# A hybrid decoder layer with one hand-placed SBUF map: no barriers, weights cast one stage ahead, the merge computed transposed

## The chip, the cores and the metric

The kernel runs on all eight cores of one Trainium2 chip, one batch element a core, no traffic between cores. The cores lie on two dies, 0 to 3 and 4 to 7. The time is the device time of the slowest core, in microseconds (us). Such a program has a second, slower state, in which the cores of a die get a lower TensorE clock.

## The reference, cut to what matters

One decoder layer over 4096 tokens of width 1024: gated linear attention (GLA, branch A) and dilated attention in three head groups (branch B) read one normalised input; a gated merge joins them; then cross-attention into 256 memory tokens, and a gated feed-forward with a short convolution. Cut marks are `...`:

```python
    xn = rms_norm(h, norm_mix)
    qa, ka, va, ra, za, qb, kb, vb = jnp.split(xn @ w_in, IN_OFFSETS, axis=-1)
    ...
    o_a = gla_chunked(heads(qa) * (GLA_DK ** -0.5), heads(ka), heads(va), heads(log_a))   # (B,H,S,dv)
    ...
    qd = rope_partial(rms_norm(dheads(qb), dil_q_norm), cos, sin)
    kd = rope_partial(rms_norm(dheads(kb), dil_k_norm), cos, sin)
    o_b = dilated_attention(qd, kd, vd).reshape(b, s, DIL_OUT).astype(dt)
    ...
    gates = jax.nn.sigmoid((xn @ w_merge_gate + b_merge_gate).astype(jnp.float32)).astype(dt)
    g_a, g_b = jnp.split(gates, 2, axis=-1)
    merged = g_a * (o_a @ w_br_gla) + g_b * (o_b @ w_br_dil)
    return h + merged @ w_mix_out
```

All weights arrive as f32; all matmuls are bf16. So each weight is converted once.

## The kernel before

Five stages, each with its own buffers, one behind the other. TensorE, VectorE (DVE), ScalarE (ACT), GpSimd (POOL) and the load queue (SP) each run their instructions in program order and wait on each other by semaphores; a helper records every operation, so the line numbers of the profile are the helper's, and tiles tell what is meant.

Weights are converted from memory to memory while GLA runs, one piece a chunk, each held by POOL until the chunk's output has been stored:

```python
        def emit_conv(after=None, n=1):
            ...
            if after is not None:
                fw.wait_for("pool", [after])
            fw.dma(d_, s_, q="pool", join=True)
        ...
        def R_t(c):                       # end of a GLA chunk
            ...
            fw.copy("act", oT[:, :, :], ptb.rearrange("p (c t) -> p c t", c=8))
            st_ins = fw.dma(oaT_d[c].rearrange("p (c t) -> p c t", c=8), oT[:, :, :], join=True)
            emit_conv(st_ins, 1)
```

Every stage ends in `fw.barrier()`: all engines wait for all engines and all transfers. The merge makes token rows, adds the gate bias as a matmul row, and transposes its result:

```python
        for kc in range(8):
            fw.mm(pg[:, :], xnv[:, kc, :], wmg[:, kc, gs_], start=(kc == 0), stop=False)
        fw.mm(pg[:, :], ones_row_b, bmg[0:1, gs_], start=False, stop=True)
        fw.act(ga[:, :], pg[:, :], AF.Sigmoid)
        ...
        for cc in range(8):
            fw.tr(ptb[:, cc * 128:(cc + 1) * 128], mr[:, cc * 128:(cc + 1) * 128], ident_b)
```

## Time and profile before

Median 3388.12 us of 3 runs (3384.28 to 3392.4). To keep books I cut the span of the profiled run at eight events, taken from their start times in the trace: the copies of a chunk's output (oT), of an attention tile's values (va), the last product of the merge (ma), the last query norm (qn) and the first copy of the feed-forward (abt).

| stretch | before, us |
|---|---|
| start to first GLA output copy | 100.9 |
| 24 GLA chunks | 458.1 |
| GLA chunk 24 to fourth attention tile | 175.8 |
| to last attention tile | 637.6 |
| to last merge product | 638.5 |
| to last query norm of cross-attention | 366.4 |
| to first feed-forward copy | 81.5 |
| to the end | 918.7 |
| span | 3377.5 |

A stretch is worth reading where TensorE is not full: rows one to three, and the places where one stage hands over to the next. The lines that carry this are in the prediction below.

### The profile page before, as it was taken

The numbers are of one execution on the slowest core, as the hardware profiler recorded it, in microseconds if no ns is written. First come the engines' busy times: TensorE is split into PE (matmuls) and PEld (weight loads), VectorE is DVE, ScalarE is ACT, GpSimd is POOL, SyncE is SP. The second block draws the span as 40 slices with busy tenths as digits, with TensorE's granted clock in tenths as the row PEclk, the third lists the DMA queues.
The fourth block names the chain that finished last, engine by engine and source line by source line (L and its number), as shares of the span: only waits on it lengthen the run. The fifth ranks groups of instructions, "written<-read, shape, count | busy, mean of one in ns | idle before, by whom it ended". The sixth has DMA issues, their size and how long they took to land.

```text
span 3377.5 us, 56089 instructions; the slowest of 8 cores (3357.1 to 3377.5 us)
## 1 busy us (share of the span) xinstructions
PE 3050.0 (90%) x18030; PEld 1535.8 (45%) x18030; DVE 1811.7 (54%) x3042; ACT 1386.0 (41%) x2679; POOL 868.2 (26%) x1284
## 2 busy tenths in 40 slices
PE   4887778699999999399999994999799999999998
PEld 2443344465555666244444442445344444444444
DVE  3665556467777767223333332576565566556554
ACT  2654445336666655234444442656321122112211
POOL 1332222236666666232222210000010011001100
PEclk8998889779999999699999997999899999999999
DMA  7678884021121111433333324134561101110110
GB/s 152 106 141 138 137 137 85 26 85 40 42 77 39 39 39 42 149 116 125 111 116 112 115 91 140 57 127 144 201 204 63 63 26 38 63 63 23 41 63 26
DMA packets 107503, 304.31 MB, mean 90 GB/s; under 512 B 12038, under 2 KB 24862, under 8 KB 104094
## 3 DMA queue, kind: packets, MB, share of 16 engines
q1 hardware_dynamic: 96702, 244.02, 21.3%
q0 software_dynamic: 8928, 50.93, 10.7%
q10 hardware_dynamic: 1584, 5.77, 0.5%
q8 instruction: 150, 2.46, 0.3%
q14 instruction: 139, 1.14, 0.1%
HBM read 258.92 MB, written 137.23 MB: 117 GB/s over the span
## 4 chain that ended last, share of the span: by engine, by line
PE 82%; DMA 7%; DVE 4%; issue 2%; ACT 2%; POOL 1%; SPq 1%; DVEq 0%; ACTq 0%; POOLq 0%
PE uP L170 27%; PE qP L170 16%; PE pj L170 15%; PE rP L170 9%; PE bP L170 6%; DMA oaT_d<-oT 4%; PE pS L170 2%; PE ptC L174 1%; PE ptC L170 1%; PE pO L170 1%; PE qP L174 1%; PE bP L174 1%; DVE on L229 1%; SPq L166 1%; PE rP L174 1%
## 5 line engine op out<-in xcount | busy, mean ns | idle before, releaser
L170 PE MATMUL uP<-x3T,wup 128*128 128x512 bf16 x2816 | 610.3, 380 | 0.0
L170 PE MATMUL pj<-wd,xnT 128*128 128x512 bf16 x2304 | 553.7, 384 | 2.1 <-DVE qg L203 2.1
L170 PEld LDWEIGHTS uP<-x3T,wup 128*128 128x128 bf16 x2816 | 275.9, 98 | 332.9 <-issue 1.7
L170 PEld LDWEIGHTS pj<-wd,xnT 128*128 128x128 bf16 x2304 | 253.0, 120 | 195.2 <-issue 8.1
L170 PE MATMUL uP<-wdn,yT 128*128 128x512 bf16 x1408 | 305.2, 379 | 0.0
L170 PE MATMUL qP<-wmg,xnT 128*128 128x512 bf16 x1024 | 241.9, 379 | 0.0
L239 POOL COPY hist<-abt 128x2 f32<-128x2 f32 x176 | 32.6, 185 | 808.2 <-ACT abt L238 808.2
L203 DVE TENSOR_TENSOR qg<-pj,gqk 128x512 f32<-128x512 f32 x192 | 132.8, 691 | 188.3 <-ACT sq L196 161.0
L170 PEld LDWEIGHTS uP<-wdn,yT 128*128 128x128 bf16 x1408 | 137.7, 98 | 166.2
L238 ACT COPY abt<-uP 128x512 f32<-128x512 f32 x176 | 100.2, 569 | 266.9 <-PE uP L170 266.9
L203 DVE TENSOR_TENSOR ma<-qP,ga 128x512 f32<-128x512 f32 x128 | 88.3, 690 | 203.0 <-ACT ga L196 200.8
L203 POOL TENSOR_TENSOR mr<-ma 128x1024 bf16<-128x1024 f32 x32 | 75.2, 2351 | 417.4 <-DVE ma L203 417.4
L196 ACT ACTIVATE pT<-pS 128x1024 bf16<-128x1024 f32 (+1 forms) x192 | 177.9, 927 | 4.5 <-PE pS L170 3.6
L196 ACT ACTIVATE sq<-pj 128x512 f32<-128x512 f32 x192 | 114.7, 599 | 151.0 <-PE pj L170 151.0
L196 ACT ACTIVATE ga<-qP 128x512 f32<-128x512 f32 x128 | 76.5, 598 | 228.1 <-PE qP L170 224.4
L203 DVE TENSOR_TENSOR h2f<-uP,h2f 128x512 f32<-128x512 f32 x64 | 44.3, 692 | 211.2 <-PE uP L170 210.4
L170 PEld LDWEIGHTS qP<-wmg,xnT 128*128 128x128 bf16 x1024 | 100.3, 98 | 120.9 <-issue 0.4
L196 ACT ACTIVATE gl<-cv_1 128x512 f32<-128x512 f32 x88 | 55.5, 631 | 222.6 <-DVE cv_1 L229 222.6
L196 ACT ACTIVATE gl<-cv_0 128x512 f32<-128x512 f32 x88 | 55.5, 631 | 219.3 <-DVE cv_0 L229 219.3
L229 DVE SCALAR_TENSOR_TENSOR cv_0<-abt,wcb,cv_0 128x512 f32<-128x512 f32 x176 | 132.2, 751 | 19.1 <-DVE cv_0 L229 0.5
L229 DVE SCALAR_TENSOR_TENSOR cv_1<-abt,wcb,cv_1 128x512 f32<-128x512 f32 x176 | 132.2, 751 | 18.3
L170 PE MATMUL bP<-wv,xnT 128*128 128x512 bf16 x512 | 132.6, 406 | 1.3 <-DVE ke_1 L203 1.3
(245 smaller groups left out, 5379.3 us busy)
## 6 DMA issues: line engine op xcount, KB each, us to landing
og_d<-og SPq DMA_DIRECT2D x96, 260.0 KB, 2.1
ogl<-og_d SPq DMA_DIRECT2D x96, 260.0 KB, 3.0
xt<-x SPq DMA_DIRECT2D x32, 512.0 KB, 7.9
xtT<-x SPq DMA_DIRECT2D x32, 512.0 KB, 4.8
h_d<-xtT SPq DMA_DIRECT2D x32, 512.0 KB, 2.9
h1x<-h_d SPq DMA_DIRECT2D x32, 512.0 KB, 5.5
h_d<-h1x SPq DMA_DIRECT2D x32, 512.0 KB, 3.6
h2f<-h_d SPq DMA_DIRECT2D x32, 512.0 KB, 6.1
```

Source lines behind the costliest of these rows:

```text
L166: return self._add(q, lambda e: e.dma_start(out=o, in_=i, **kw), [in_], [out], dma=True, join=join)
L170: return self._add("pe", lambda e: e.matmul(o, l, r, start=start, stop=stop), [lhsT, rhs], [out], xr=xr)
L174: return self._add("pe", lambda e: e.transpose(o, i, d), [in_, ident], [out])
L196: return self._add("act", lambda e: e.activation(o, i, func, **kw), reads, writes, xr=xr, xw=xw)
L203: return self._add(eng, lambda e: e.tensor_tensor(o, a, b, op), [in0, in1], [out], xr=xr)
L229: return self._add(eng, lambda e: e.scalar_tensor_tensor(o, a, scalar, b, op0, op1), reads, [out])
L238: return self._add("act", lambda e: e.copy(o, i), [in_], [out])
L239: return self._add(eng, lambda e: e.tensor_copy(o, i), [in_], [out])
```

## The change

Intent: one table of addresses in SBUF (the core's on-chip memory) for the whole kernel, in which each weight has a place that falls free one stage before it is needed. Then weights can be loaded with the conversion done on the way (called a cast from here on), a stage ahead; no barrier is needed, because each buffer inherits the waits of what lay there; and the tail of a stage can be interleaved with the head of the next. Besides, the merge makes its output already transposed (the bias is then one number per partition and rides in the activation), and the rotary tables are computed inside GLA. The host also lays weights and positions out in the order in which the loads take them, which the cuts below do not show.

The diff is long; its core, cuts marked:

```diff
+    def at(self, name, shape, dt, off):
+        assert off % 32 == 0
+        return self.register(Buf(self.handle(name, shape, dt, off), name), off, self.nbytes(shape, dt))
...
-            emit_conv(st_ins, 1)
...
-        emit_conv(None, 1000)
-        fw.barrier()
...
+        if c == NT - 1:                  # inside the last GLA chunk
+            c_alloc()                    # attention's buffers; load_wd(1), then gqk
+            for j in range(3):
+                proj(0, j)
+        R_on(c)
+        if c == NT - 1:
+            rope(0)
...
+        if c == 27:
+            c_early()                    # first attention weights wd0, tables
...
-                        fw.mm(pg[:, :], ones_row_b, bmg[0:1, gs_], start=False, stop=True)
-                        fw.act(ga[:, :], pg[:, :], AF.Sigmoid)
...
+        for kc in range(8):
+            fw.mm(pg[:, :], sl[:, gb + kc, :], xn[s_][:, kc, :], start=(kc == 0), stop=(kc == 7))
+        sg = T1["sg"].next()
+        fw.act(sg[:, :], pg[:, :], AF.Sigmoid, bias=bmg[:, br * 8 + m:br * 8 + m + 1])
...
+    kv_plan = {(4, 1): [lambda: kv_alloc(0), kv_alloc2, lambda: kv_norm(0)],
...
+        if 6 <= k < 19:
+            up_load(k - 6)
```

(`...` cuts; comments on the cut lines are mine.)

## The prediction

> **What bounds the kernel now.** I read the page first, to see which engine is full and where. Its slices, one digit for 84.4 us of the 3377.5 us span:
>
> ```profile
> PE   4887778699999999399999994999799999999998
> ...
> PEclk8998889779999999699999997999899999999999
> ```
>
> TensorE is full in the long stretches and holds a full clock there; it falls short in slices 1 to 8 and in dips at slices 9, 17, 25 and 29. The dips are the seams between stages, each behind a barrier. The view of busy time by stretch says whether another engine is near its limit (columns: stretch, length, then busy us of PE, weight loads, DVE, ACT, POOL, then granted clock, DMA share, GB/s):
>
> ```profile
> 320.00:392.00 72.00, 48.33 (x273) 25.16 (x272) 35.17 (x65) 25.51 (x58) 15.28 (x22) 0.83 0.86 136
> 559.00:615.00 56.00, 51.33 (x301) 26.63 (x302) 35.61 (x72) 28.19 (x66) 16.53 (x16) 1.00 0.10 30
> 900.00:1000.00 100.00, 100.00 (x905) 56.43 (x904) 72.13 (x130) 65.27 (x102) 67.22 (x85) 1.00 0.23 73
> 1600.00:1700.00 100.00, 100.00 (x523) 44.61 (x523) 35.82 (x53) 42.61 (x64) 24.58 (x16) 1.00 0.37 119
> ```
>
> These are the linear attention (GLA) with weight conversion running, the same four chunks' work without it, the dilated attention, and the merge. Attention and merge are TensorE at 100%. In GLA nothing is full while conversion runs, and TensorE takes 51 of 56 us when it has stopped. Who waits there is in the view of waits for 110 to 645 us:
>
> ```profile
> DVE on L229 <- POOL hs L203: 67.0, 20, 9.3
> POOL nss L221 <- ACT junkA L196: 83.9, 19, 7.6
> POOL w_ffn_up_bf L166 <- DMA oaT_d<-oT: 38.1, 3, 15.8
> ```
>
> POOL stands before a conversion's issue until the store of the chunk's output has landed (24 such issues), and DVE then waits for the small POOL results queued behind. The seams are in TensorE's own waits over the whole span:
>
> ```profile
> PE qP L174 <- DVE obn L203: 43.8, 1, 43.8
> PE uP L174 <- DMA crow<-b_ffn_conv: 24.3, 1, 24.3
> PE ptC L170 <- DMA prow<-positions: 18.6, 1, 18.6
> ```
>
> One wait each: the first tile of the merge, of the feed-forward, and of the rotary tables. Last, the chain that ended last gives the rhythm of one merge tile (start, length):
>
> ```profile
> 1500.81 13.67 PE qP L170 x60
> 1515.04 3.45 PE qP L170 x16
> 1519.16 13.67 PE qP L170 x60
> ```
>
> A tile repeats every 18.35 us. Sixteen matmuls of 512 columns take 3.45 us, 0.2156 each: the unit of all sums below.
>
> **What the Trainium skill says.** "TensorE: Matmul & The Clock Gate", part 1 ("What's actually happening"): the PE clock is half by default and activity releases it. The trace agrees: 0.50 in the seam 2432 to 2456, 0.83 in the stalled GLA stretch, 1.00 in full ones. So a filled gap also speeds up the matmuls after it. The same page (under "Seeing it yourself") says that dense matmuls on several cores pull a die to 13/16. The trace disagrees: eight cores at 1.00 from 2500 to 3200; I budget the full clock. "DMA: Bandwidth & Descriptors", "SWDGE vs HWDGE vs iDMA": a transfer that casts must be issued from GpSimd. Here all weight conversions are POOL issues; the new kernel therefore still queues every weight on POOL, in order with its arithmetic. "ScalarE: Activation LUTs", "What ACT_TABLE_LOAD costs": 1283 ns; the trace has 10 loads in 100 us of merge, 12.8 us. The change takes the Ln/Exp pair out of the merge and so most of these, but ACT is at 43% there: worth nothing directly.
>
> **The change, part by part** (us of the profiled span).
>
> *Start.* DVE does nothing useful until 25.2, when the slow load of the gate bias lands (11.2 us). The new kernel takes that bias from a transposed table and starts the weight loads before any barrier. The last bound is then the 128 KB norm load, about 16. **-9.**
>
> *GLA loop.* From the first output copy (100.9) to that of chunk 24 (559.0): 458 us for six groups of four chunks, 67 to 87 each. The group without conversion takes 56.0 (559.04 to 615.05), but it also has no input normalisation: 4 x 8 transposes at 0.056 = 1.8 on TensorE, and 4 x (0.75+1.22) = 7.9 on DVE, which had 20 us free. I take 59.5 a group: 357. The conversion leaves the loop entirely. The rotary tables come in: 20 DVE passes over 768 columns (0.29 us at 256 columns, 0.42 for the two-input form, so some 0.6 and 1.0), 15 us on a DVE that is at 80%; +8. **-93.**
>
> *GLA to attention.* Last store 643.9; at 717.1 TensorE has done 1.33 attention tiles (9.3 us at 7.0). 64 us lost to barrier, positions load and 42.9 us of table matmuls. Now the first projection is inside the last chunk and its weights were loaded four chunks earlier. Some 3 us stay; the 6 us idle in the last chunk shrink by 3. **-64.**
>
> *Attention.* 96 tiles at some 7.0 us, TensorE 100%. The group order changes, not the work. Combining the group outputs of the first eight tiles adds 2 x 1.29 us of POOL every third tile (67% busy) and 0.25 us of TensorE: nothing visible. **0.**
>
> *Attention to merge.* Last attention matmul 1390.4, first merge matmul 1434.4: 44, and some 5 idle in the drain. Now three blocks of the merge run in the drain. Their weights (slabs of 0.92 MB in bf16) are there, but slabs 3 to 7 and the output weights can only be loaded when attention's buffers die. At some 2 MB per 20 us (the conversions' landing times) a slab takes 9 us, a block is computed in 28 x 0.2156 = 6.0. Slab 3 lands before it is needed, slab 7 and the output weights some 5 late. I leave 8 us of stall. **-41.**
>
> *Merge, transposed.* Before: 76 matmuls of which 4 are bias rows, and 20 transposes. 56 of the 60 in 13.67 us make 12.07, so the bias rows cost 1.6. After: 56 + 16 matmuls and 12 transposes: 12.07 + 3.45 + 0.73 = 16.25. 32 x 2.1 = 67 gained. Given back: the single activation buffer, 1 MB, is reloaded between groups with about 8 us of other work to hide it; 7 x 1 = 7. The drain of the old merge (2021.6 to 2030.6) is filled: 8. **-68.**
>
> *Merge to cross-attention.* 2030.6 to 2089.8 = 59; the memory keys' matmuls stay, 64 x 0.2156 + 2 = 16, but run inside the merge. **-43.** The head's steps (7.4 us with 4 us of matmuls) now hold the last four merge outputs, **-10.**
>
> *Cross-attention to feed-forward.* 2430.6 to 2455.5: no matmul. Up-weights 0 to 16 and the first activations are now loaded earlier. Five up-weights and all of the down-weights (5.8 MB) still start at this seam; the latter are needed 76 us later and take some 65. I leave 4. **-21.** The feed-forward itself is 176 x 24 x 0.2156 = 911 in both.
>
> Sum: 9+93+64+41+68+43+10+21 = 349; 3377.5 - 349 = 3029. The median of the timed runs lies 10.6 above the profiled span: **3040**.
>
> **Rivals.** *POOL takes the barriers' place.* All weights are in POOL's in-order queue; an issue whose target is not yet free holds up every POOL addition behind it, as the oaT wait does today. For it: that very wait. Against: most targets die one stage ahead, and POOL is at 25% in merge and 0 in cross-attention. If each of six reloads stopped TensorE for 10 us: 3100. *DVE becomes the GLA bound.* With tables and normalisation it has some 46 to 53 us of a 59 us group. If groups take 66 us: 3080. *The conversion was not what slowed GLA*, but latency between engines: then groups stay at 70 or more and 3110 follows. Against: the group without it, 56 us, at clock 1.00. *Loads were hidden anyway*: true in attention and feed-forward, refuted at the seams by TensorE's waits. Only the slow state of a die would make it slower than before.
>
> **Range and chances.** Of the sum, 281 us are in the seams and GLA and rest on measured idle time, 68 on the merge and counted matmuls. A large rewrite usually finds waits that I do not see, so the high side is longer: 2985 (GLA at TensorE's 55 us a group, no stalls) to 3110 (one rival true, or two halved). Two per cent faster means below 3320, which needs only a fifth of the sum: 0.96.
>
> **What would show it.** GLA groups of 57 to 62 us between output copies, no POOL wait for the oaT store; no TensorE wait over 10 us after 60 us; merge at 65 us per four tiles; PEclk 9 in nearly every slice after the third; TensorE 96% busy or more. Wrong if: POOL shows long waits before slab or up-weight issues and TensorE waits for them; or GLA groups stay near 70 with DVE over 90%.

## More of the kernel before

The chunk loop, the part that one experiment reorders (c is the chunk; the steps of chunk c+1 are begun while c ends):

```python
        R_o(c); ...; R_r(c + 1); nscale(i); R_on(c)
        for h in hs_: P_qk(s_ + 1, h)     # queries, keys of the next 4 chunks
        R_v(c + 1, 0)                     # values, first half
        R_a(c + 1)                        # key-query product: needs ke from DVE
        R_v(c + 1, 1)                     # values, second half
        nstat(i + 1); ntrans(i); nload(i + 3); R_t(c)
```

## The result, and the profile after

The changed kernel takes 3182.95 us (median of 4 runs, 3179.71 to 3186.26); the kernel before took 3388.39 beside it. The ratio of the fast runs is 0.9394, 95% interval 0.9378 to 0.941. Ratios here are the mean time of one kernel's fast runs over that of the other's in the same rounds, so not quite the ratio of the medians quoted. Executions in which one die ran at a lower clock are left out of the means. The direction was right, but the time lies above the range of 2985 to 3110: 205 us gained of 348 predicted.

The same books, with the prediction's terms put into the rows that they belong to (us of the profiled span; the 8 us of the old merge's drain fall behind its last product, so in the next row):

| stretch | before | predicted | after | after less predicted |
|---|---|---|---|---|
| start to first GLA output copy | 100.9 | 91.9 | 107.3 | +15 |
| 24 GLA chunks | 458.1 | 365.1 | 400.2 | +35 |
| GLA chunk 24 to fourth attention tile | 175.8 | 111.8 | 140.7 | +29 |
| to last attention tile | 637.6 | 637.6 | 641.2 | +4 |
| to last merge product | 638.5 | 537.5 | 570.4 | +33 |
| to last query norm | 366.4 | 305.4 | 331.1 | +26 |
| to first feed-forward copy | 81.5 | 60.5 | 65.8 | +5 |
| to the end | 918.7 | 918.7 | 921.4 | +3 |
| span | 3377.5 | 3028.5 | 3178.1 | +150 |

The page's slices after (79.5 us a digit; the last row is the load of the 16 DMA engines):

```profile
PE   3888898599999999899899887999899999999998
...
PEclk9999999799999999999999999999999999999999
DMA  7111111511131322544545439446810110110110
```

The clock row is 9 in every slice but the eighth, and TensorE is full in more of them. It still dips; set the DMA row under the dips: slices 8 and 20 (5 and 5), 25 and 29 (9 and 8). At 25 and 29 the DMA engines are near full; at 8 and 20 they are half busy, as in other slices that do not dip, so the row alone does not tell the cause. TensorE's own waits over the span, with total, times and longest (L245 to L318 are the helper's lines here):

```profile
PE psum L249 <- DVE on_109 L304: 38.9, 4, 32.9
PE psum L249 <- DVE xsT_202 L296: 20.1, 3, 15.9
...
PE psum L249 <- DMA grow<-b_gla_gate: 16.3, 1, 16.3
```

The 43.8, 24.3 and 18.6 of before are gone. Two new single waits have come, of 32.9 and 15.9; the third, for the gain rows at the start, was 11.0 before. The first names DVE, but DVE itself stood. In the order of time around the seam from GLA to attention (start, length, and in brackets the engine's idle time before it and what ended it):

```profile
589.99 0.72 SPq L241 DMA_DIRECT2D gqk<-dil_k_norm  x1
592.55 2.24 POOL L241 DMA_DIRECT2D wd_170<-w_dil  x4
623.47 0.69 DVE L278 TENSOR_TENSOR qg_139<-psum,gqk 128x512 f32<-128x512 f32 x1 [30.53 <-DMA gqk<-dil_k_norm]
```

A small load (gqk, the norm weights of queries and keys, two loads of 256 KB) is issued 2.6 us before the 3 MB cast of the second attention weights, which land after 41 us. DVE stands 30.5 us for it, and `on_109`, the output of the last GLA chunk, is behind it in DVE's order: so TensorE stands 32.9.

It is tempting to blame the cast, but the traces say otherwise for this load. The kernel before issues the same two loads at 646.5 and 661.1. There the first landed after 14.5 us, with only 16 KB of positions beside it; both were hidden, because DVE first used them at 716.2, behind the table matmuls. Landing of the first, and busy time by stretch while it was under way (columns as in the prediction):

```profile
DMA to landing us min/median/max: 14.5/14.5/14.5
```

```profile
648.00:660.00 12.00, 0.00 (x0) 0.00 (x0) 0.00 (x0) 0.00 (x0) 0.00 (x0) 0.50 0.07 20
```

In the changed kernel the cast, though issued at 592.6, moves no packet until 604, and gqk goes no faster for that:

```profile
592.00:604.00 12.00, 3.90 (x19) 1.81 (x16) 0.94 (x5) 1.19 (x2) 3.12 (x11) 0.88 0.06 18
```

With the DMA engines 6 to 7% busy it moves at 18 to 20 GB/s, 68 to 76 pieces of 256 bytes a us. By an estimate from that rate, its 2048 pieces take 27 to 30 us alone; from issue to DVE's start it took 33.9. So most of this wait is the load's own form and its late issue; only the 4 to 7 us left over can be the cast's.

The second wait, 15.9 us, does have a cast beside it. It is in the merge's fifth group, where the memory tokens are loaded:

```profile
1573.21 0.74 SPq L241 DMA_DIRECT2D mt<-mem  x1
1574.36 0.63 POOL L241 DMA_DIRECT2D wkv_204<-w_xkv  x1
1590.56 1.06 ACT L271 ACTIVATE junkT<-mt 128x1024 bf16<-128x1024 f32 x1 [17.20 <-DMA mt<-mem]
```

Here the DMA engines are full: from 1580 to 1590 the casts' queue moved 1.69 MB and the fast queue 0.46. The second tile of the memory, loaded when this cast had landed, took 3.7 us. And in the head of cross-attention, where the casts of the output weights (wxo) and up-weights have just been issued, DVE stands for the store of a tile's transposed activations (x2s):

```profile
1916.79 1.22 DVE L278 TENSOR_TENSOR x2s_203<-psum,gall 128x1024 bf16<-128x1024 bf16 x1 [9.38 <-DMA xn_d<-x2s_203]
```

In GLA no transfer is named. Busy time by stretch (stretch, length, busy us of PE, weight loads, DVE, ACT, POOL, then clock, DMA share, GB/s), first group of four chunks and third:

```profile
107.29:180.60 73.31, 60.36 (x345) 31.23 (x349) 52.18 (x95) 41.39 (x87) 26.75 (x30) 0.93 0.13 44
...
249.90:313.80 63.90, 57.38 (x346) 30.18 (x350) 43.70 (x81) 37.83 (x84) 21.98 (x24) 0.98 0.15 50
```

DVE is at 68% in the third group and the DMA engines at 15%: neither is full, and TensorE is busy 57.4 of 63.9 us.

### The profile page after: what moved, and what is told of

Its sections match the earlier page's. It is cut to its first block, busy times and chain, and to the rows that moved or that the text cites. A ratio compares the mean times of both kernels' runs of the same rounds, so it can differ in the third digit from the quotient of the medians.

```text
span 3178.1 us, 54582 instructions; the slowest of 8 cores (3162.8 to 3178.1 us)
## 1 busy us (share of the span) xinstructions
PE 2904.7 (91%) x17139; PEld 1465.6 (46%) x17454; DVE 1845.5 (58%) x2994; ACT 1290.9 (41%) x2521; POOL 946.6 (30%) x1434
## 4 chain that ended last, share of the span: by engine, by line
PE 71%; DVE 10%; issue 6%; ACT 6%; DMA 6%; SPq 0%; POOL 0%; DVEq 0%; ACTq 0%; POOLq 0%
PE psum L245 68%; PE psum L249 3%; ACT jh L271 1%; DMA gqk<-dil_k_norm 1%; DMA xt_61<-x 1%; DVE on_109 L304 1%; ACT junkX L271 1%; DMA oat<-oaT_d 1%; DMA x2i_214<-xn_d 1%; DVE cm_68 L308 1%; DMA mt<-mem 1%; DMA gon<-gla_out_norm 1%; ACT L271 0%; DVE x3s_240 L314 0%; DVE qn_2_222 L304 0%
## 5 line engine op out<-in xcount | busy, mean ns | idle before, releaser
L245 PE MATMUL psum<-wdn,yT 128*128 128x512 bf16 x1379 | 303.7, 379 | 3.0 <-DVE yT L278 1.5
L245 PEld LDWEIGHTS psum<-wdn,yT 128*128 128x128 bf16 x1408 | 137.7, 98 | 167.9 <-issue 2.0
L245 PE MATMUL psum<-wd_170,xnT 128*128 128x512 bf16 x736 | 176.7, 382 | 6.6 <-issue 6.6
L245 PE MATMUL psum<-wd_135,xnT 128*128 128x512 bf16 x737 | 176.4, 382 | 5.1 <-issue 4.9
L245 PE MATMUL psum<-wd_171,xnT 128*128 128x512 bf16 x736 | 175.2, 380 | 3.3 <-issue 2.4
L313 ACT COPY abt_279<-psum 128x512 f32<-128x512 f32 x88 | 50.1, 569 | 242.3 <-PE psum L245 235.8
L271 ACT ACTIVATE gl_278<-cv_1_274 128x512 f32<-128x512 f32 x88 | 55.4, 630 | 223.7 <-DVE cv_1_274 L304 223.7
L271 ACT ACTIVATE gl_277<-cv_0_273 128x512 f32<-128x512 f32 x88 | 55.4, 630 | 218.5 <-DVE cv_0_273 L304 218.5
L278 DVE TENSOR_TENSOR qg_139<-psum,gqk 128x512 f32<-128x512 f32 x96 | 66.2, 689 | 110.5 <-ACT sq_137 L271 69.9
L245 PEld LDWEIGHTS psum<-wd_170,xnT 128*128 128x128 bf16 x768 | 103.0, 146 | 48.0
L278 DVE TENSOR_TENSOR qg_140<-psum,gqk 128x512 f32<-128x512 f32 x96 | 66.1, 689 | 89.6 <-ACT sq_137 L271 60.3
L245 PEld LDWEIGHTS psum<-wd_135,xnT 128*128 128x128 bf16 x768 | 81.2, 115 | 67.7 <-issue 1.9
L245 PEld LDWEIGHTS psum<-wd_171,xnT 128*128 128x128 bf16 x768 | 68.5, 98 | 74.7
L296 DVE TENSOR_SCALAR cv_0_273<-abt_279,gall 128x512 f32<-128x512 f32 x88 | 48.1, 546 | 77.6 <-ACT abt_279 L313 77.6
L271 ACT ACTIVATE sq_138<-psum 128x512 f32<-128x512 f32 x96 | 57.5, 599 | 84.4 <-PE psum L245 84.4
L296 DVE TENSOR_SCALAR cv_1_274<-abt_280,gall 128x512 f32<-128x512 f32 x88 | 48.1, 547 | 73.6 <-ACT abt_280 L313 73.6
L278 POOL TENSOR_TENSOR ogl_172<-ogl_172 128x520 f32<-128x520 f32 x64 | 84.4, 1319 | 9.4 <-DMA ogl_172<-og_d 4.8
L271 ACT ACTIVATE sq_137<-psum 128x512 f32<-128x512 f32 x96 | 57.4, 598 | 61.1 <-PE psum L245 60.9
```

The lines of the kernel that those rows point to most:

```text
L245: return self._add("pe", lambda e: e.matmul(o, l, r, start=start, stop=stop), [lhsT, rhs], [out], xr=xr)
L271: return self._add("act", lambda e: e.activation(o, i, func, **kw), reads, writes, xr=xr, xw=xw)
L278: return self._add(eng, lambda e: e.tensor_tensor(o, a, b, op), [in0, in1], [out], xr=xr, xw=xw)
L296: return self._add(eng, lambda e: e.tensor_scalar(o, a, s1, s2, op0, **kw), reads, writes)
L313: return self._add("act", lambda e: e.copy(o, i), [in_], [out])
```

## The experiments

**Theory A**: what was freed is partly given back to transfers issued just in time. They share the DMA engines with cast-loads that start at the same moment in the freed space, and engines that work in order stand behind them. **Theory B**: what is left in GLA is no transfer but short waits between engines, in the order in which TensorE meets them. The rivals of A: the seams are long by their own chains of dependent steps, or by the barriers, and the transfer only came last by chance. A third rival was not on the list when the runs were planned: a small load is slow by itself and only issued too late. For gqk the traces above decide for it. All edits are on the changed kernel except where it is said.

### 1. The small load earlier

```diff
+    def gqk_early():                     # at chunk 28 instead of 31
+        CC["gqk"] = ar.at("gqk", (128, 2, 8, 64), F32, 150 * K_)
+        ... same two loads ...
+        if c == 28:
+            gqk_early()
```

> Edit: the norm-weight tile gqk of the dilated attention is loaded three chunks earlier (its place is free by then), no longer in the same chunk as the 3 MB cast-load of wd1. In the changed kernel DVE stands 30.5 us for it. Theory A (just-in-time loads on the fast queue share the DMA engines with cast-loads issued at the same moment, and engines in order stand behind them): that wait falls below 2 us, last GLA store to fourth attention tile falls from 140.7 by 22 to 30 us, the ratio to the kernel before from 0.939 to about 0.931. Rival (the seam is long because the first attention tile's chain of engines is long, the DMA only happened to be the last of them): another wait of 15 us or more takes its place and the total falls by less than 10 us.

Only one of the four executions was fast, 3170.41 us, so there is no ratio; its profile has span 3168.9, 9 us below the changed kernel. The stretch from GLA chunk 24 to the fourth attention tile fell from 140.7 to 121.7. DVE's largest wait there is now another, of 10.5 us:

```profile
DVE qg L278 <- ACT sq L271: 45.5, 30, 10.5
```

The load itself took 29.5 us to land (last figure of the transfer line):

```profile
gqk<-dil_k_norm SPq DMA_DIRECT2D x1, 256.0 KB, 29.5
```

So the late load held 19 us of the seam, less than the 22 that A expected at least, and no wait of 15 us took its place, as the rival had it. That a neighbour made the load slow is not shown by this run: it now starts beside the cast of the first attention weights, but from 578 to 588 that cast had landed and gqk still moved at 16 GB/s with the DMA engines 6% busy. The merge and tail stretches were 6 and 2 us longer than in the changed kernel's profile. Run 3, which does not touch the merge either, has 5 us more there too: such differences lie between runs, so stretches are compared and not spans.

### 2. The start

```diff
-    for h in range(4): ... wqk[h] cast          # all eight casts at once
-    for j in range(4): ... wvr[j] cast
-    fw.ts("dve", gon[:, :], gon[:, :], 0.5, ALU.mult)    # ahead of the norm loop
+        if i < 4:  qk_load(i)                   # behind the statistics of tile i
+        elif i < 6: vr_load(2 * i - 8); vr_load(2 * i - 7)
+    fw.ts("dve", gon[:, :], ...)                # behind the norm loop
```

> Edit: the casts of wqk are issued behind the statistics of input tiles 0 to 3, those of wvr behind tiles 4 and 5, and the halving of the output-norm row moves behind the norm loop, so DVE no longer stands for its 17 us load. Theory A: the loads of the first input tiles and of the gain rows land in 8 us or less instead of 10 to 17, TensorE's waits before 60 us (52 us) fall by 10 to 18, first output copy at 90 to 97 us instead of 107. Rival (the start is bound by the weights themselves, whenever they are issued): the wait moves to the first products with wqk or wvr and the first output copy stays within 4 us of 107.

Ratio 0.9366 (0.9347 to 0.9385). On core 2 (die 0, clock 0.978, span 3164.6) the first output copy is at 96.0 us instead of 107.3. The landing times (last column, median us from issue) of the changed kernel, then of this one:

```profile
xt_61<-x SPq DMA_DIRECT2D x4, 512.0 KB, 10.0
...
gon<-gla_out_norm SPq DMA_DIRECT2D x1, 128.0 KB, 17.1
```

```profile
wvr<-w_gvr POOLq DMA_DIRECT2D x4, 1024.0 KB, 16.8
...
gon<-gla_out_norm SPq DMA_DIRECT2D x1, 128.0 KB, 6.4
```

The weights land in 16.8 us (median of four) instead of 30 to 45, and the small load in 6.4 instead of 17.1, though all the bytes are the same. A holds: 11.3 us, within what it expected. The edit does two things, though: it paces the casts, and it takes DVE's wait for gon (the output-norm row) out of the way of the norm loop; their shares were not separated. That the casts held the small loads up is seen in the changed kernel's trace: from 12 to 24 us the casts' queue moved 1.80 MB and the fast queue 0.18.

### 3. GLA: order alone

```diff
             R_v(c + 1, 0)
-            R_a(c + 1)
             R_v(c + 1, 1)
+            R_a(c + 1)
```

> Edit: in the GLA chunk loop only the order of three steps: both value projections of the next chunk come before its key-query product, instead of the product between them. No transfer changes. Theory B (what is left in a GLA group, 64 us against the 59.5 predicted, is TensorE in order behind short waits on DVE and ACT results: ke_3 2.6, vs_0 1.7 in the group looked at): groups fall by 2 to 4 us, the whole by 12 to 25 us. If what is left is DMA or clock (theory A alone): no group changes by more than 0.5 us.

Ratio 0.9323 (0.9304 to 0.9341), median of the fast runs 3156.4: 27 us faster than the changed kernel. The 24 chunks take 376.1 us instead of 400.2, each group 3 to 5 us less. TensorE's waits in the third group of the changed kernel:

```profile
PE psum L245 <- DVE ke_3_88 L278: 2.6, 1, 2.6
PE psum L245 <- ACT vs_0_95 L313: 1.7, 1, 1.7
PE psum L249 <- DVE qe_1_82 L304: 1.0, 1, 1.0
```

This run's third group by busy time, and TensorE's waits for DVE's keys in it:

```profile
239.30:300.20 60.90, 56.23 (x344) 29.65 (x348) 43.74 (x82) 37.94 (x85) 22.15 (x24) 1.00 0.15 53
```

```profile
PE psum L245 <- DVE ke L278: 0.8, 1, 0.8
```

With 3.6 us of value products between the keys and their use, DVE has made `ke` in time; the waits fall by some 2 us, and TensorE's busy time by another 1.2, at a clock of 1.00 instead of 0.98. B holds: 24 of GLA's 35 us were order, not traffic.

### 4. The tables

```diff
-        for f_ in tab_ops[5 * c:5 * c + 5]: f_()
+        if c == 0: tab_ops[0](); fw.memset("pool", tab[:, :, :], 0.0)
```

> Edit, with a wrong result on purpose: the rotary tables are not computed (zeros are stored), nothing else changes. If the tables' DVE passes are what makes the first two GLA groups 73.3 and 69.3 us instead of the 64 of the later ones, both fall to 63 to 66 us, together 13 to 16 us less (predicted cost of the tables: 8). If it is the start-up itself, or the weight casts still landing, they stay above 68.

The result is wrong on purpose, and one of two executions was fast. The first two groups take 67.1 and 64.2 us instead of 73.3 and 69.3: 11.4 us for the tables where 8 was predicted; the 3 us by which the first group still exceeds the second are not theirs.

### 5. The memory tokens, and the last group's activations

```diff
-    kv_plan = {(4, 1): [lambda: kv_alloc(0), kv_alloc2, lambda: kv_norm(0)], ...
+    kv_plan = {(4, 0): [kv_alloc2],      # both memory tiles loaded here, two places
+               (4, 2): [lambda: kv_alloc(0), lambda: kv_norm(0)], ...
-               (6, 6): [kv_wxq]}
+               (7, 1): [kv_wxq]}
```

> Edit: in the merge, both tiles of the memory are loaded into their own places one to two blocks before they are normalised (in the changed kernel: one place, loaded in the step that uses it, 17.2 us while the cast of wkv runs), wkv's cast starts one block later and the query weights' cast moves from the block that reloads the 1 MB activations of the last group to two blocks later. Theory A: the eight blocks that hold the memory load fall from 85 us to about 70, the wait of 7.6 us for the activations of the last group goes: the whole falls by 16 to 24 us. Rival (those blocks are long because of their extra products and chains on ACT and DVE, the transfer only happened to come last): less than 8 us.

Ratio 0.9293 (0.9189 to 0.9397; wide, because two of the fast runs of the kernel before were near 3405 and 3435). The stretch to the last merge product is 541.2 us instead of 570.4 (on core 1), 29 less and more than A's 16 to 24: the eight blocks with the memory load take 67.0 instead of 85.0, and in the last group the wait for the reloaded activations is gone (33.2 for four blocks instead of 43.7). ACT's largest waits over these groups, before and after the edit:

```profile
ACT junkT L271 <- DMA mt<-mem: 24.4, 2, 17.2
```

```profile
ACT junkT L271 <- DVE xtT L278: 33.5, 6, 6.2
```

No transfer is left among them. The edit loads earlier, into two places, and moves two casts; which of these did how much was not separated.

### 6. The head, a miss

```diff
+    x2r.items.append(rx.sb("x2s1", (128, 8, 128), BF16))      # second buffer
-        if 6 <= k < 19: up_load(k - 6)
+        if 6 <= k < 32 and k % 2 == 0:                        # held by POOL
+            fw.copy("pool", pace[:, 0:8], TC[k - 1]["qn"][:, 0:8])
+            up_load((k - 6) // 2)
-            if k == 3: kv_wxo()
+            if k == 4: (held likewise) kv_wxo()
```

> Edit: in the cross-attention head a second buffer for the transposed activations on their way out, and the cast-loads of wxo and of the up-weights are held by POOL until the tile before has been normalised, one up-weight every second tile instead of six at once. Theory A: the 9.4 us wait of DVE for the store of x2s and TensorE's 9.3 and 3.1 us behind it go; last merge product to last query norm falls from 331 to about 317, the whole by 10 to 18 us. Rival (the head is a long chain of dependent steps, the transfers only fill it): falls by under 5 us.

Nothing: ratio 0.9395. DVE's wait for the store is gone as foreseen, but TensorE waits as long for something else. Its wait, for the activations of a tile on their way back in (x2i), and the landing of those loads:

```profile
PE psum L245 <- DMA x2i<-xn_d: 12.0, 2, 7.6
```

```profile
DMA to landing us min/median/max: 2.5/8.1/14.6
```

The trace shows why: the cast of wxo, moved one step later, was now issued 2.5 us before the load of the sixth tile's activations, which then took 14.6 us where the quickest took 2.5. By its number the rival had won; but the victim had only changed. So the next edit was made to tell these apart.

### 7. The head again

```diff
+        if k + 2 < NT: x2load(k + 2)         # top of the step, ahead of the stores
+            if k < 4: wxo_part(k)            # wxo in four pieces, one a step
     (second buffer and held up-weights as in 6)
```

> The first head edit gained nothing: the wait of DVE for the store went, but the next activation load, issued 2.5 us after the cast of wxo, then landed 14.6 us later and TensorE stood 7.6 us for it. Edit: second buffer as before, wxo's cast in four pieces, one behind each of the last four merge outputs, activation loads issued at the top of each step instead of behind a store, up-weights one every second tile. Theory A: no TensorE wait over 4 us in the head, last merge product to last query norm 331 to 315-322, the whole 8 to 16 us less. Rival (the head is bound by its chain of dependent steps whatever the loads do): under 4 us less.

The stretch to the last query norm is 323.0 us (core 1) against 331.1, with 30.5 instead of 40.2 for the second four tiles; the ratio, 0.9336, has too wide an interval (0.9195 to 0.9477) to say it. TensorE's largest waits, on core 6, whose stretch is 322.3:

```profile
PE psum L249 <- DVE xsT L296: 4.2, 2, 3.5
PE psum L245 <- DMA x2i<-xn_d: 3.7, 1, 3.7
```

8 to 10 us of A's claim are shown here by the trace alone (in the profiles of runs that leave the head alone the stretch is 330 to 334); the rest of the head's miss is not, nor which of the four changes did it.

### 8. The kernel before without its pacing

```diff
-            emit_conv(st_ins, 1)
+            emit_conv(None, 1)
```

> Edit on the kernel before: its weight conversions no longer wait for the store of the chunk's output (that wait is pacing, not data); everything else is as it was. If POOL's stand before each conversion is what stretched the GLA groups of the kernel before (67 to 87 us), the groups fall to near the 64 of the changed kernel and the kernel before gets 40 us or more faster. If the traffic of the conversions, or latency between engines, stretched them, it changes by less than 15 us or gets slower, because more conversions pile up at once.

It gets slower, by little: ratio 1.0133 (1.0021 to 1.0245, so unclear by the 2% that verdicts here ask for), 3441 to 3447 us in the fast runs. The groups take 64, 79, 94, 124, 88 and 82 us. The worst one by busy time, and one of the largest waits of the third and fourth groups:

```profile
338.80:462.40 123.60, 67.37 (x374) 33.74 (x372) 47.51 (x90) 38.09 (x84) 24.90 (x31) 0.81 0.83 114
```

```profile
ACT oT L238 <- DMA oaT_d<-oT: 91.4, 4, 33.4
```

ACT stands up to 33.4 us for the store of a chunk's output, which shares the queues with the piled-up conversions. POOL's wait, which I had read as the brake, was a governor. That speaks for taking the conversions themselves out of GLA, as the change does; and A was already at work in the kernel before. (This shows that more conversions at once are worse; a run without any was not made.)

### 9 and 10. Barriers back

```diff
+        if c == NT - 1:                  # behind R_t of the last chunk
+            fw.barrier(); c_alloc(); ...; rope(0)
+        if step == N_ + 3: fw.barrier()  # attention | merge
+    fw.barrier()                         # merge | cross-attention
+    fw.barrier()                         # cross-attention | feed-forward
```

> Undo one part of the change: a barrier of all engines and transfers at each of the four seams (GLA to attention, with the first attention tile behind it; attention to merge; merge to cross-attention; cross-attention to feed-forward). Loads one stage ahead, conversions gone, transposed merge stay. If the barriers themselves with the cold start after each are what the seams of the kernel before cost: 60 to 110 us more than the changed kernel, 15 to 30 at each seam. If the loads ahead brought the gain and the barrier by itself costs little: under 30 us more.

Ratio 0.9634, median 3254.1 us. But the last barrier stood behind the issue of the down-weights' casts and waited for these too: the stretch to the first feed-forward copy grew by 42 us. Again with that barrier ahead of the casts:

> The barriers again; in the first try the one before the feed-forward also waited for the 5.8 MB of down-weights, cast just ahead of it, and that stretch grew by 42 us. Now it stands before these loads are issued. If a barrier and the cold start behind it are what costs: that stretch still grows by 12 to 30 us, the whole is 45 to 65 above the changed kernel. If it was the wait for the down-weights: it grows by less than 8 us and the whole is 30 to 42 above.

Ratio 0.949 (0.9429 to 0.955), fast runs 3219.55 to 3222.57: 38 us above the changed kernel, span 43 above. By stretch: GLA to attention +15, merge +4, cross-attention's head +8, feed-forward's head +19. The stretch in question fits the first theory (12 to 30), the total lies between the two. The identical barrier at the first seam cost 29 in run 9 and 15 in run 10, so single seams are good to some 15 us. In the merge, profiles of kernels that leave it alone lie from 565 to 576 us, so its +4 is not readable. At the first seam the late load is there with the barrier too. DVE's wait in run 10:

```profile
DVE qg L278 <- DMA gqk<-dil_k_norm: 41.4, 1, 41.4
```

So the barrier comes on top of a seam that the load already holds up. Here too the load is slow alone: from 634 to 642 us, the cast having landed, it moves at 12 GB/s with the DMA engines 4% busy. What the barrier would cost with that load out of the way was not run.

### 11. Five edits together

Runs 1, 2, 3, 5 and 7, and a second buffer for oT.

> The five edits that gained, together: gqk three chunks earlier, paced start, value projections before the key-query product, memory tiles and last activations clear of the casts, head with spread wxo cast; and a second buffer for the chunk output on its way to memory, because after the gqk edit TensorE stood 7.8 us for ACT, which stood for that buffer's store. One by one the stretches they touch fell by 18.5, 11.3, 25, 29.5 and 10 us, 94 in sum. If the causes are separate (theory A plus B): 3075 to 3100 us, a ratio of 0.908 to 0.916, and TensorE busy 96% or more of the span. If they are one chain that only moves its wait: above 3120.

Ratio 0.918 (0.9156 to 0.9204), fast runs 3096.73 to 3114.57. Between the two: 75 us gained of 94. Core 4 held its clock up to the feed-forward (1.00 from 2000 to 2050 us), so what lies before can be read. GLA and merge stretches have what the single runs gave (375.8 and 542.0); the seam has 126.3, more than run 1 alone. DVE's wait there:

```profile
DVE qg L278 <- DMA gqk<-dil_k_norm: 24.3, 1, 24.3
```

GLA now runs faster into it, and the two loads took 28.8 and 45.1 us. At first wd0 (the first attention weights) and the tables are in flight beside them, but from 540 to 548 us they move alone, at 19 GB/s with the DMA engines 7% busy.

### 12. And the small load small

```diff
+        CC["gqk"] = ar.at("gqk", (128, 2, 64), F32, (ar.size - 512) // 32 * 32)
+            fw.dma(CC["gqk"][:, a_, :], dram_bc(SM[nm], 64), join=True)    # at chunk 8
-   ... CC["gqk"][:, j, :, :], ALU.mult
+   ... CC["gqk"][:, j, :].raw(0, [[0, 8], [1, 64]]), ALU.mult
     (gain rows issued ahead of input tiles 1 and 2)
```

> The combination before gained less than the sum of its parts at the seam from GLA to attention: there the early gqk load shared the queues with wd0 and the tables (issued one chunk earlier) and landed after 29 and 45 us, so DVE still stood 24 us. Edit: gqk is loaded at the ninth chunk, as 64 numbers a row instead of 512 (the eight heads read the same ones), and the gain rows at the very start are issued ahead of the second and third input tile; the rest as in the combination. Theory A: the wait of DVE for gqk is gone, the seam (GLA chunk 24 to fourth attention tile) falls from 126 to 105-112 us, the whole from 3108 to 3080-3095. Rival (the first attention tile's chain fills the seam anyway): seam stays above 120, whole above 3100.

3068.5 us (6 runs, 3066.27 to 3078.06), ratio 0.9043 (0.8999 to 0.9087): better than A expected and faster than both kernels. The seam takes 102.7 us, less than the 111.8 predicted; the first copy comes at 90.4. The two small loads land in 4.1 and 4.4 us, and 300 us before they are used. A quiet moment alone would not have made them so short: the first full-sized one took 14.5 us in the quiet of the kernel before. Some 3 us of the seam's gain belong to run 3's order, which also shortens the last eight chunks; what the second oT buffer does there was not run alone. The page:

```profile
PE 2918.1 (95%) x17454; PEld 1462.2 (48%) x17454; DVE 1847.9 (60%) x2994; ACT 1291.6 (42%) x2521; POOL 953.8 (31%) x1449
...
PE   4889999999999999899999989997999999999998
...
PEclk8999999999999999999999999999999999999999
```

The dip of slice 8 is gone. TensorE's largest waits are now in the start (27.5 us in eight pieces for the scaled input, 9.7 for the gain rows) and small ones in GLA.

## Why the prediction was wrong

The books once more, with run 12:

| stretch | predicted | after | run 12 | edits that closed it |
|---|---|---|---|---|
| start | 91.9 | 107.3 | 90.4 | paced casts (-11), gain rows first |
| 24 GLA chunks | 365.1 | 400.2 | 376.0 | order (-24) |
| GLA to attention | 111.8 | 140.7 | 102.7 | small load earlier and smaller, order (-3) |
| attention | 637.6 | 641.2 | 641.4 | |
| merge | 537.5 | 570.4 | 544.3 | memory and activations earlier (-29) |
| cross-attention | 305.4 | 331.1 | 324.0 | spread casts (-8) |
| feed-forward head | 60.5 | 65.8 | 70.0 | |
| feed-forward | 918.7 | 921.4 | 921.4 | |
| span | 3028.5 | 3178.1 | 3070.2 | |

**The step that failed** is the overlap that the working took for granted at every seam. It followed the weights and asked for each whether it would land in time ("its weights were loaded four chunks earlier. Some 3 us stay"; "Up-weights 0 to 16 and the first activations are now loaded earlier"). Every smaller load and store it took as hidden. The weights did land in time; small transfers did not, for two reasons:

- *Beside casts.* At the start, at the memory tokens and in the head, small loads and stores issued with a cast landed after 12 to 18 us. Runs 2, 5 and 7, which move transfers and change no bytes of them, give back 11, 29 and 8 us.
- *By its own form.* gqk takes some 27 to 30 us with nothing beside it (estimate above), and the working did not have it at all. Run 1 gives back 19 us by loading it earlier, run 12, with it early and small, all of the seam's 29.

The other failed step is the size of the GLA group: 24 us of order and 3 of tables.

**Start (-9 predicted, +6 came).** The term took the 128 KB norm load to be the last bound at 16 us. It landed at 25, because the weight loads that start "before any barrier" ran beside it.

**GLA (-93 predicted, -58 came).** The mis-sized term is the group, "I take 59.5": it added the normalisation's 1.8 us of TensorE to the 56.0, and 1.7 more, and believed DVE's spare time would hide the rest. Measured 62.9 to 65.7; run 3 gives 59.7 to 61.1 by order alone. The prediction's third rival (latency between engines) was thus true in kind, at 4 us a group, where it had been given 10 or more. Tables: 8 predicted, 11.4 measured. Some 8 us of the stretch stay open.

**GLA to attention (-64, -35 came).** Barrier, table matmuls and positions load are gone, as foreseen. "Some 3 us stay" failed by one 30.5 us wait for gqk. The kernel before had that load in the same stretch, hidden under the table matmuls; taking these away laid it bare. With it out of the way, run 12 gains 9 us more than predicted here, 3 of them by run 3's order.

**Merge (-101 in the two terms of this stretch, -68 came).** The transposed merge itself is as counted: four token tiles take 33.3 + 32.4 = 65.7 us, predicted 65. The miss is the wait for the memory tokens and for the last reload of the activations, and run 5 closes 29 of 33. That reload was in the working at 1 us a group; it was 7.6 in the one group that a cast shared.

**Cross-attention's head (-61, -35 came).** Run 7 closes 8 to 10 of the 26. The rest is open: in run 12 the later tiles too are 1 to 2 us longer per four than in the kernel before (82 against 79.7 for eight).

**Feed-forward's head (-21, -16 came).** Not tested by an edit of its own; the waits there are for the load of h1 and the store of x3 beside the last up-weights, with the DMA engines 86% busy.

**The rivals.** None reached the measured 3182.95. "POOL takes the barriers' place" (3100) was wrong in its engine: POOL does not hold TensorE up in the changed kernel; transfers on SP's queue do, beside POOL's casts or, for gqk, by themselves. Latency between engines (3110) was nearest in number; it was real, at 4 us a group, but the groups did not stay at 70. "DVE becomes the GLA bound": no, 44 of 64 us. "Hidden anyway": at the seams neither, as runs 9 and 10 show: the barriers alone are worth some 40 us.

**What would show it.** Of its own list the prediction failed on GLA groups (57 to 62 foretold), on "no TensorE wait over 10 us after 60 us" (32.9 and 15.9) and on TensorE at 96% (91%; 95% in run 12). It held on POOL, on the clock row and on the merge's 65 us. One reading of the page was off: it lists a dip at slice 9, where the PE row has 9 and only the clock row is low; TensorE's own dip is slice 8, with 6. No sum rests on it.

## What to carry to other kernels

Before you call a transfer hidden, ask two things, and of the small ones as well as of the weights. How long does it take with nothing beside it? gqk, in 2048 pieces, needed some 27 to 30 us, and only a longer wait in the kernel before had covered it. And what lies beside it? A load moved ahead is free for its reader and not for its neighbours: for each large cast, list the small loads and stores issued within its landing time and which in-order engine stands behind each; move those first, or pace the cast in pieces. When a wait is removed and the time stays, look for the same wait under another name (run 6) before you believe the rival. And before you remove a wait that looks like a brake, ask whether it paces something (run 8).

## What the Trainium skill lacked or had wrong

- "DMA: Bandwidth & Descriptors", section "Queues, rings and completion order", says that each DMA engine takes turns between the queues that have work, a packet at a time. The trace agrees: from 1580 to 1590 us of the changed kernel the casts' queue moved 103 packets and the fast queue 128, but 1.69 MB against 0.46. No page says what that does to a small transfer: a 256 KB load landed in 2.5 us at best and in 14.6 behind a cast of wxo (run 6); a 256 KB store took 2.1 us in the median of run 6, where the casts are held, and 11.9 beside them in the changed kernel.
- The same page, "Specifications", asks for 512 bytes or more a piece for full speed, but does not say how slow smaller pieces are. The norm weights were read in pieces of 256 bytes and moved at 12 to 20 GB/s with the DMA engines 4 to 8% busy and no cast beside them (kernel before, changed kernel, runs 1, 10 and 11). All 128 rows also read the same 256 bytes; which of the two slows them was not separated.
- "TensorE: Matmul & The Clock Gate", section "Seeing it yourself", expects 13/16 of the clock whenever three or more cores of a die run dense matmuls. In such dense stretches only slow runs show that here: in the slow profile of run 11, core 4 had 0.81 from 2600 to 3200 us. In run 12, fast, all eight cores had a mean of 0.988 to 0.993, with TensorE busy 95% of the span on the slowest.
- No page gives the cost of a barrier of all engines and transfers between the stages of a kernel: four of them cost 38 to 43 us here (run 10).
